# The second MLP product of five chunks: seven products instead of eight for the latents' two token tiles

## The chip, the cores and the metric

The kernel runs on one core of a Trainium2 chip. The metric is the device time of one execution in microseconds (us). Each time before is one of three runs; the profile is of one further execution of the same program.

## What is computed

The reference is one step of a flow-matching backbone: a token-mixing layer (an mLSTM and a pooling mixer), then an MLP. There are 128 prompt tokens and 256 latent tokens, D = 2048, and the MLP has 8192 hidden units. The change lies in the MLP:

```python
x = x + gate_a * _rmsnorm(mix, norm_w[1])
h = _rmsnorm(x, norm_w[2]) * (1 + scale_f) + shift_f
y = jnp.square(jax.nn.relu(h @ w1)) @ w2
x = x + gate_f * _rmsnorm(y, norm_w[3])
```

All of it is in fp32. The conditioning vectors (shift, scale, gate) are products of two vectors with a matrix of 2048 x 12288, one of which, gate_f, is worked out while the MLP runs.

## The kernel before

The 384 tokens are three token tiles of 128: tile 0 is the prompt, tiles 1 and 2 are the latents. TensorE multiplies in fp32r, a reduced format, so every operand is split into a high and a low part, hi and lo, and each product is three matmuls: high by high, high by low, low by high. For a weight tile this is `load_w`: a DMA brings 512 KB into a raw buffer (three of them), ScalarE copies it to hi (line 126), VectorE subtracts hi from raw to get lo (line 127); hi and lo have four buffers each.

The MLP runs in 8 chunks of 1024 hidden units (eight contraction tiles of w2). `gemm_T` on w1 makes a group of 256 hidden units, transposed: four loads, 24 matmuls of 384 columns for each (lines 135 to 137), and then for each of the two hidden tiles `evac_normed`: Relu on ScalarE (805), the square on VectorE (806), and `split_T` into hid high and low (181 and 182). `mlp_out(ch)` is the second product of a chunk: four blocks n of 512 output columns, in each four loads of two contraction tiles by 512 columns, and for each load 2 x 3 x 3 matmuls of 512 columns (901 to 903) with the hidden tile as the stationary operand, into three PSUM banks, one for each token tile. After a block three VectorE additions bring the banks into y (925; copies in chunk 0, 923).

The order is: one w1 group of the next chunk, the second product of this chunk, three more w1 groups. TensorE, ScalarE and VectorE each take their instructions in the order in which the scheduler has put them, which follows the order of the program and readiness. Side work is fed in between the loads by `Feed`: with rate r it takes r steps after each load. `ff` brings gate_f, at rate 0.2, so that it is spread from chunk 0 to chunk 6 (line 268 does its VectorE steps of 512 columns, one for each of the weight rows that a DMA has brought); `fx` stores an intermediate for the residual in chunk 0 (876), and `fn` (`norm_h2`) works the shift into h in chunk 0 (795 to 800). The last chunk ends with `last_part`, in which the third token tile's last 512 columns go in two halves of 256.

## Time and profile before

| | us |
|---|---|
| median of three runs (lowest, highest) | 1732.19 (1730.23, 1733.49) |
| the profiled execution's own time | 1733.51 |
| its span | 1731.8 |
| TensorE busy | 1693.1 |
| VectorE busy | 1082.6 |
| ScalarE busy | 629.1 |

Read it by stage: TensorE's share is an average over the token mixing, where it waits now and then, and the MLP, of which a table by stretches tells more than the page. In the stretches each number with (x) behind it is busy time and instructions of an engine, in the order of the first line; then come the granted TensorE clock (1.00 is the full one) and the DMA's share. In a timeline a matmul's length includes time in which the next already runs, so its cost is read from start to start.

### The profile page before, as it was taken

The numbers are of one execution on the slowest core, as the hardware profiler recorded it, in microseconds if no ns is written. First come the engines' busy times: TensorE is split into PE (matmuls) and PEld (weight loads), VectorE is DVE, ScalarE is ACT, GpSimd is POOL, SyncE is SP. The second block draws the span as 40 slices with busy tenths as digits, with TensorE's granted clock in tenths as the row PEclk, the third lists the DMA queues.
The fourth block names the chain that finished last, engine by engine and source line by source line (L and its number), as shares of the span: only waits on it lengthen the run. The fifth ranks groups of instructions, "written<-read, shape, count | busy, mean of one in ns | idle before, by whom it ended". The sixth has DMA issues, their size and how long they took to land.

```text
span 1731.8 us, 24241 instructions
## 1 busy us (share of the span) xinstructions
PE 1693.1 (98%) x9461; PEld 1527.8 (88%) x9461; DVE 1082.6 (63%) x1620; ACT 629.1 (36%) x1050; POOL 150.6 (9%) x186
## 2 busy tenths in 40 slices
PE   6999999999999999999999999999999999999997
PEld 3777899989999989989988988988988988998986
DVE  3676749898989959997347443466434344443446
ACT  4332345545433335553322332332332332332332
POOL 0000001221001224530000000000000000000100
PEclk9999999999999999999999999999999999999999
DMA  9978858777778894755446444454444445434543
GB/s 303 308 254 290 281 155 257 234 236 241 221 234 266 261 309 125 210 164 173 131 123 193 151 131 122 126 156 144 122 128 128 122 122 180 124 122 143 175 133 109
DMA packets 235266, 320.71 MB, mean 185 GB/s; under 512 B 14368, under 2 KB 177808, under 8 KB 234768
## 3 DMA queue, kind: packets, MB, share of 16 engines
q1 hardware_dynamic: 227760, 303.61, 56.1%
q0 software_dynamic: 5728, 13.69, 2.8%
...
q8 instruction: 74, 1.21, 0.3%
...
## 4 chain that ended last, share of the span: by engine, by line
PE 76%; DVE 9%; DMA 8%; issue 4%; ACT 1%; POOL 1%; SPq 0%; DVEq 0%; ACTq 0%; POOLq 0%
PE y L901 10%; PE y L903 10%; PE y L902 10%; PE acc_w L135 9%; PE acc_w L136 9%; PE acc_w L137 9%; DVE ada_acc L268 4%; DMA raw_u<-in_w_in_dram 3%; PE acc_o L135 1%; PE acc_o L137 1%; PE acc_o L136 1%; PE acc_q L135 1%; PE acc_q L137 1%; DMA raw_v<-in_w_in_dram 1%; PE acc_q L136 1%
## 5 line engine op out<-in xcount | busy, mean ns | idle before, releaser
L127 DVE TENSOR_TENSOR lo_w<-raw_w,hi_w 128x1024 fp32r<-128x1024 f32 x256 | 313.2, 1224 | 402.5 <-ACT hi_w L126 402.1
L126 ACT ACTIVATE hi_w<-raw_w 128x1024 fp32r<-128x1024 f32 x256 | 271.3, 1060 | 560.9 <-PE y L903 277.6
L136 PE MATMUL acc_w<-h2l,hi_w 128*128 128x384 f32 (+1 forms) x1024 | 345.8, 338 | 0.5 <-DVE h2l L857 0.5
L135 PE MATMUL acc_w<-h2h,hi_w 128*128 128x384 f32 (+1 forms) x1024 | 344.6, 338 | 1.6 <-ACT h2h L853 1.2
L137 PE MATMUL acc_w<-h2h,lo_w 128*128 128x384 f32 (+1 forms) x1024 | 345.4, 337 | 0.0
L268 DVE SCALAR_TENSOR_TENSOR ada_acc<-ada_raw,sg,ada_acc 128x1024 f32<-128x1024 f32 (+1 forms) x240 | 258.2, 1111 | 0.8 <-DMA ada_raw<-in_ada_w_dram 0.7
L135 PEld LDWEIGHTS acc_w<-h2h,hi_w 128*128 128x128 f32 x1024 | 192.2, 188 | 3.5 <-ACT h2h L853 2.0
L136 PEld LDWEIGHTS acc_w<-h2l,hi_w 128*128 128x128 f32 x1024 | 192.8, 188 | 1.8 <-DVE h2l L857 0.8
L137 PEld LDWEIGHTS acc_w<-h2h,lo_w 128*128 128x128 f32 x1024 | 192.5, 188 | 0.1
L806 DVE TENSOR_TENSOR z<-z 128x384 f32<-128x384 f32 x54 | 30.0, 555 | 53.4 <-ACT z L805 53.2
L126 ACT ACTIVATE hi_wo<-raw_wo 128x1024 fp32r<-128x1024 f32 x32 | 34.0, 1062 | 80.4 <-DMA raw_wo<-in_w_out_dram 57.6
L925 DVE TENSOR_TENSOR y<-y,y 128x512 f32<-128x512 f32 x81 | 55.5, 691 | 11.1 <-PE y L903 10.8
...
L805 ACT ACTIVATE z<-acc_w 128x384 f32<-128x384 f32 x54 | 26.3, 488 | 75.5 <-PE acc_w L137 75.5
L394 PE MATMUL v<-hi_v,hh 128*128 128x384 f32 (+1 forms) x144 | 49.0, 341 | 0.0
L395 PE MATMUL v<-lo_v,hh 128*128 128x384 f32 (+1 forms) x144 | 47.9, 332 | 0.0
L396 PE MATMUL v<-hi_v,hl 128*128 128x384 f32 (+1 forms) x144 | 47.8, 332 | 0.0
L221 PE MATMUL ada<-ada_raw,cT 128*32 128x256 f32 x672 | 45.7, 392 | 1.6 <-DMA ada_raw<-in_ada_w_dram 1.5
L127 DVE TENSOR_TENSOR lo_wo<-raw_wo,hi_wo 128x1024 fp32r<-128x1024 f32 x32 | 40.2, 1265 | 9.8 <-ACT hi_wo L126 9.7
L135 PE MATMUL acc_k<-hh,hi_k 128*128 128x384 f32 x128 | 44.4, 347 | 0.8 <-ACT C L603 0.8
L135 PE MATMUL acc_o<-hh,hi_o 128*128 128x384 f32 x128 | 44.1, 345 | 0.0
L135 PE MATMUL acc_q<-hh,hi_q 128*128 128x384 f32 x128 | 44.0, 343 | 0.0
...
## 6 DMA issues: line engine op xcount, KB each, us to landing
raw_w<-in_w_dram SPq DMA_DIRECT2D x256, 512.0 KB, 3.7
ada_raw<-in_ada_w_dram SPq DMA_DIRECT2D x188, 512.0 KB, 4.8
raw_wo<-in_w_out_dram SPq DMA_DIRECT2D x32, 512.0 KB, 5.1
raw_u<-in_w_in_dram SPq DMA_DIRECT2D x16, 512.0 KB, 8.8
raw_q<-in_w_in_dram SPq DMA_DIRECT2D x16, 512.0 KB, 5.1
raw_k<-in_w_in_dram SPq DMA_DIRECT2D x16, 512.0 KB, 5.0
raw_o<-in_w_in_dram SPq DMA_DIRECT2D x16, 512.0 KB, 4.9
...
```

The lines of the kernel that those rows point to most:

```text
L126: nc.scalar.activation(hi[:, 0:n], raw[:, 0:n], AF.Copy)
L127: low = lambda: nc.vector.tensor_tensor(lo[:, 0:n], raw[:, 0:n], hi[:, 0:n].bitcast(F32), op=ALU.subtract)
L135: nc.tensor.matmul(ps, lh, rh, start=start, stop=False)
L136: nc.tensor.matmul(ps, lh, rl, start=False, stop=False)
L137: mm3.ins = nc.tensor.matmul(ps, ll, rh, start=False, stop=stop).ins
L268: nc.vector.scalar_tensor_tensor(acc[:, g, :], raw[:, a, :], cj, acc[:, g, :], op0=ALU.mult, op1=ALU.add)
L394: nc.tensor.matmul(acc[i][:, 0:n], xh[:, sl], hi[:, k, :], start=k == 0, stop=False)
L395: nc.tensor.matmul(acc[i][:, 0:n], xh[:, sl], lo[:, k, :], start=False, stop=False)
L901: nc.tensor.matmul(acc, xh[:, s], hi, start=k == 8 * ch, stop=False)
L902: nc.tensor.matmul(acc, xh[:, s], lo, start=False, stop=False)
L903: nc.tensor.matmul(acc, xl[:, s], hi, start=False, stop=k == 8 * ch + 7)
L925: nc.vector.tensor_tensor(dst, acc[i], dst, op=ALU.add)
```

## The change

In chunks 2 to 6 the second product is no longer `mlp_out` but `mlp_seven`. For each pair of contraction tiles (an even and an odd one) and each pair of column halves (256 each) the latents' two token tiles form a 2 x 2 product of 2 x 2 blocks. Strassen's scheme (in Winograd's form) needs seven block products for it where the plain way needs eight; the prompt's tile stays plain and shares weight sums with them. So the loads become four tiles of 4 x 256 columns (b11, b21, b22, b12), three of seven weight operands are the raw tiles b11, b21, b22, and four are differences: t1 = b12 - b11, t3 = b22 - b12, t2 = b22 - t1, t4 = b21 - t2, worked out in place on VectorE. All seven are split into hi and lo. The hidden side's sums are made in `evac_pair`, with a third split (`hs`) for each pair of hidden tiles. A block has 132 matmuls of 256 columns instead of 72 of 512, five PSUM banks, and six additions into y and into two running sums r16 and r7, which `seven_done` folds into y after chunk 6.

To make room, gate_f is finished before chunk 2: its rate goes from 0.2 to 0.65, with buffers in a pool of its own that is closed there. The tail's buffers open in chunk 7, `z` has five buffers for two, and the masks and a few tiles move to other pools. Within a chunk from 2 on the order is: blocks 0 and 1, one w1 group, blocks 2 and 3, three w1 groups.

```diff
-N_X = 2
+N_X = 4
+RATE_GF = 0.65
+S_FIRST, S_LAST = 2, 6
...
+    def evac_pair(t, ps):
+
+        z = mlp.tile([P, NTOK], F32, tag="z", name=f"z{t}", bufs=5)
+        nc.scalar.activation(z, ps[:, 0:NTOK], AF.Relu)
+        nc.scalar.activation(z, z, AF.Square)
+        if t % 2 == 0:
+            z_even.append(z)
+            return
+        z0, s = z_even.pop(), mlp.tile([P, NTOK], F32, tag="z", name=f"s{t}", bufs=5)
+        a11, a21, a12, a22 = z0[:, P:2 * P], z0[:, 2 * P:], z[:, P:2 * P], z[:, 2 * P:]
+        s1, s2, s4 = (s[:, i * P:(i + 1) * P] for i in range(3))
+        tt = nc.vector.tensor_tensor
+        tt(s1, a21, a22, op=ALU.add)
+        tt(a21, a11, a21, op=ALU.subtract)
+        hid[t - 1], hid[t] = split_T(z0, f"hid{t - 1}"), split_T(z, f"hid{t}")
+        tt(s2, s1, a11, op=ALU.subtract)
+        tt(s4, a12, s2, op=ALU.subtract)
+        hid["s", t] = split_T(s, f"hs{t}")
...
-    fx, ff, fn = Feed(first_side(), 1.0), Feed(gate_late(), 0.2), Feed(norm_h2(), 1.0)
+    fx, ff, fn = Feed(first_side(), 1.0), Feed(gate_late(), RATE_GF), Feed(norm_h2(), 1.0)
...
+    def mlp_seven(ch, n, strp, r16, r7):
...
+        for m, (r, c) in enumerate(((0, 0), (1, 0), (1, 1), (0, 1))):
+            pool, tag = ((wp, "raw"), (strp, "raw2"))[m % 2]
+            raws[r, c] = pool.tile([P, 1024], F32, tag=tag, name=f"w2_{ch}_{n}_{r}{c}", bufs=3)
+            nc.sync.dma_start(raws[r, c].rearrange("p (j q) -> p j q", q=256),
+                              w2v[:, k0 + r:k0 + 8:2, c0 + 256 * c:c0 + 256 * c + 256])
...
+        def product(m, half, row, tok, w, start=True, stop=True, js=range(4)):
...
+                nc.tensor.matmul(acc, xh, wh, start=start and j == 0, stop=False)
+                nc.tensor.matmul(acc, xh, wl, start=False, stop=False)
+                nc.tensor.matmul(acc, xl, wh, start=False, stop=stop and j == 3)
...
+        wa, wb = split(b11, "b11"), split(b21, "b21")
+        for js in ((range(3), range(3, 4)) if n == 0 else (range(4),)):
+            product("x7", 0, 0, 0, wa, js=js)
+            product("16", 0, 0, 1, wa, js=js)
+            product("yz", 0, 1, 0, wb, js=js)
+            product("23", 0, 1, 1, wb, js=js)
+        tt(b11, b12, b11, op=ALU.subtract)
+        yx = ys[0].rearrange("p (a q) -> p a q", a=2)
+        tt(yx, banks["x7"][:, 0:256].unsqueeze(1).to_broadcast([P, 2, 256]), yx, op=ALU.add)
+        w = split(b22, "b22")
+        product("yz", 1, 1, 0, w, stop=False)
+        product("23", 1, 2, 2, w)
+        tt(b12, b22, b12, op=ALU.subtract)
+        w = split(b11, "t1")
+        product("yz", 1, 0, 0, w, start=False)
+        product("45", 1, 2, 0, w)
+        tt(b22, b22, b11, op=ALU.subtract)
+        w = split(b12, "t3")
+        product("x7", 1, 0, 2, w)
+        add(ys[1], "23")
+        tt(b21, b21, b22, op=ALU.subtract)
+        w = split(b22, "t2")
+        product("16", 1, 2, 1, w)
+        add(ys[0], "yz")
+        w = split(b21, "t4")
+        product("45", 0, 1, 2, w)
...
+            add(r7[:, n], "x7", 1)
+            add(r16[:, n], "16")
+        add(ys[2], "45")
...
+            if ch == S_FIRST:
+                ff.finish()
+                gate_scope.close()
...
+            for n in range(4):
+                mlp_seven(ch, n, strp, r16, r7)
+                if n == 1:
+                    w1_group(4 * ch + 4)
+            if ch == S_LAST:
+                for n in range(4):
+                    seven_done(n, r16, r7)
+                str_scope.close()
+            for g in range(1, 4):
+                w1_group(4 * ch + 4 + g)
```

How it moves instructions is seen at three places. On TensorE, the second product of a middle chunk before, where the second block begins (y_1_0 is the PSUM bank of token tile 0, hi_w_24 and lo_w_24 the split weights, hid24h and hid24l the hidden tile's parts):

```order
L901 MATMUL y_0_2_10557<-hi_w_30_0_10632,hid31h 128x512
L902 MATMUL y_0_2_10557<-lo_w_30_0_10633,hid31h 128x512
L903 MATMUL y_0_2_10557<-hi_w_30_0_10632,hid31l 128x512
L901 MATMUL y_1_0_10657<-hi_w_24_1_10662,hid24h 128x512
L902 MATMUL y_1_0_10657<-lo_w_24_1_10663,hid24h 128x512
L903 MATMUL y_1_0_10657<-hi_w_24_1_10662,hid24l 128x512
L901 MATMUL y_1_1_10658<-hi_w_24_1_10662,hid24h 128x512
L902 MATMUL y_1_1_10658<-lo_w_24_1_10663,hid24h 128x512
L903 MATMUL y_1_1_10658<-hi_w_24_1_10662,hid24l 128x512
```

The same engine after, at the end of the second block of chunk 4, where the products with t2 (bank 16) give way to those with t4 (bank 45):

```order
L1088 MATMUL y_1_16_12420<-hi_1_t_12557,hs37h 128x256
L1089 MATMUL y_1_16_12420<-lo_1_t_12558,hs37h 128x256
L1090 MATMUL y_1_16_12420<-hi_1_t_12557,hs37l 128x256
L1088 MATMUL y_1_16_12420<-hi_1_t_12557,hs39h 128x256
L1089 MATMUL y_1_16_12420<-lo_1_t_12558,hs39h 128x256
L1090 MATMUL y_1_16_12420<-hi_1_t_12557,hs39l 128x256
L1088 MATMUL y_1_45_12422<-hi_1_t_12574,hid33h 128x256
L1089 MATMUL y_1_45_12422<-lo_1_t_12575,hid33h 128x256
L1090 MATMUL y_1_45_12422<-hi_1_t_12574,hid33l 128x256
L1088 MATMUL y_1_45_12422<-hi_1_t_12574,hid35h 128x256
L1089 MATMUL y_1_45_12422<-lo_1_t_12575,hid35h 128x256
L1090 MATMUL y_1_45_12422<-hi_1_t_12574,hid35l 128x256
```

The matmuls are half as wide, and each group of three belongs to one of five banks.

On VectorE, a block before, around the additions of one block and the lo parts for the next:

```order
L925 TENSOR_TENSOR y_6313<-y_1_0_9671,y_6313 128x512
L925 TENSOR_TENSOR y_6314<-y_1_1_9672,y_6314 128x512
L925 TENSOR_TENSOR y_6315<-y_1_2_9673,y_6315 128x512
L127 TENSOR_TENSOR lo_w_22_2_9857<-raw_w_22_2_9854,hi_w_22_2_9856 128x1024
L127 TENSOR_TENSOR lo_w_16_3_9893<-raw_w_16_3_9890,hi_w_16_3_9892 128x1024
L127 TENSOR_TENSOR lo_w_18_3_9917<-raw_w_18_3_9914,hi_w_18_3_9916 128x1024
L127 TENSOR_TENSOR lo_w_20_3_9941<-raw_w_20_3_9938,hi_w_20_3_9940 128x1024
L925 TENSOR_TENSOR y_6313<-y_2_0_9779,y_6313 128x512
L925 TENSOR_TENSOR y_6314<-y_2_1_9780,y_6314 128x512
L925 TENSOR_TENSOR y_6315<-y_2_2_9781,y_6315 128x512
L127 TENSOR_TENSOR lo_w_22_3_9965<-raw_w_22_3_9962,hi_w_22_3_9964 128x1024
```

VectorE after, in the second block of chunk 4 (w_4_1_rc are raw tiles, in place of which the differences are written; lo_1_b and lo_1_t are lo parts of raw tiles and of differences):

```order
L1113 TENSOR_TENSOR w_4_1_01_12416<-w_4_1_11_12414,w_4_1_01_12416 128x1024
L1077 TENSOR_TENSOR lo_1_t_12511<-w_4_1_00_12410,hi_1_t_12510 128x1024
L1117 TENSOR_TENSOR w_4_1_11_12414<-w_4_1_11_12414,w_4_1_00_12410 128x1024
L1077 TENSOR_TENSOR lo_1_t_12540<-w_4_1_01_12416,hi_1_t_12539 128x1024
L1121 TENSOR_TENSOR w_4_1_10_12412<-w_4_1_10_12412,w_4_1_11_12414 128x1024
L1094 TENSOR_TENSOR y_6319<-y_1_23_12421,y_6319 128x512
L1077 TENSOR_TENSOR lo_1_t_12558<-w_4_1_11_12414,hi_1_t_12557 128x1024
L1094 TENSOR_TENSOR y_6318<-y_1_yz,y_6318 128x512
L1077 TENSOR_TENSOR lo_1_t_12575<-w_4_1_10_12412,hi_1_t_12574 128x1024
L132 TENSOR_TENSOR lo_w_5120_0_12598<-raw_w_5120_0_12595,hi_w_5120_0_12597 128x1024
L1094 TENSOR_TENSOR r_9598<-y_1_x_12418,r_9598 128x256
L1094 TENSOR_TENSOR r_9597<-y_1_16_12420,r_9597 128x512
```

Between two lo parts there stands now a difference or an addition from PSUM.

On VectorE in chunk 0's second product, before, around the lo part of the second load of block 2 (lo_w_2_2):

```order
L876 STREAM_TRANSPOSE x1b_7728<-mo_6305 128x384
L800 SCALAR_TENSOR_TENSOR h2l_6632<-h2n_7734,mod,h2h_6631 128x128
L800 SCALAR_TENSOR_TENSOR h2l_6632<-h2n_7734,mod,h2h_6631 128x256
L796 TENSOR_TENSOR h2n_7771<-h2n_7771,r2bc 128x384
L127 TENSOR_TENSOR lo_w_2_2_7781<-raw_w_2_2_7778,hi_w_2_2_7780 128x1024
L800 SCALAR_TENSOR_TENSOR h2l_6727<-h2n_7771,mod,h2h_6726 128x128
L795 TENSOR_TENSOR h2n_7802<-h2h_6743,h2l_6744 128x384
L800 SCALAR_TENSOR_TENSOR h2l_6727<-h2n_7771,mod,h2h_6726 128x256
L796 TENSOR_TENSOR h2n_7802<-h2n_7802,r2bc 128x384
L923 COPY y_6313<-y_1_0_7584 128x512
L923 COPY y_6314<-y_1_1_7585 128x512
L923 COPY y_6315<-y_1_2_7586 128x512
```

And after:

```order
L803 TENSOR_TENSOR h2n_7772<-h2n_7772,r2bc 128x384
L953 COPY y_6318<-y_1_0_7616 128x512
L953 COPY y_6319<-y_1_1_7617 128x512
L807 SCALAR_TENSOR_TENSOR h2l_6640<-h2n_7772,mod,h2h_6639 128x128
L807 SCALAR_TENSOR_TENSOR h2l_6640<-h2n_7772,mod,h2h_6639 128x256
L953 COPY y_6320<-y_1_2_7618 128x512
L273 SCALAR_TENSOR_TENSOR ada_acc_512_7335<-ada_raw_512_6_7723,sg,ada_acc_512_7335 128x512 x4
L802 TENSOR_TENSOR h2n_7815<-h2h_6734,h2l_6735 128x384
L132 TENSOR_TENSOR lo_w_2_2_7825<-raw_w_2_2_7822,hi_w_2_2_7824 128x1024
L803 TENSOR_TENSOR h2n_7815<-h2n_7815,r2bc 128x384
L273 SCALAR_TENSOR_TENSOR ada_acc_512_7335<-ada_raw_512_7_7809,sg,ada_acc_512_7335 128x512
L807 SCALAR_TENSOR_TENSOR h2l_6735<-h2n_7815,mod,h2h_6734 128x128
```

Here lo_w_2_2 has moved behind the copies of block 1 and behind four steps of the gate (ada_acc), and more of these steps follow it.

## Rows read from the trace of the kernel before

**Rows 1.** The page's header and its busy times by engine.

```profile
span 1731.8 us, 24241 instructions
PE 1693.1 (98%) x9461; PEld 1527.8 (88%) x9461; DVE 1082.6 (63%) x1620; ACT 629.1 (36%) x1050; POOL 150.6 (9%) x186
```

**Rows 2.** Table by stretches of the MLP, TensorE, VectorE and the rest.

```profile
core 0: us, PE busy (x) PEld busy (x) DVE busy (x) ACT busy (x) POOL busy (x), PEclk, DMA share, GB/s
729.40:796.30 66.90, 66.90 (x292) 54.49 (x291) 65.84 (x120) 31.39 (x54) 17.05 (x28) 1.00 0.62 178
796.30:864.66 68.36, 68.36 (x390) 68.12 (x389) 30.01 (x35) 22.35 (x29) 0.00 (x0) 1.00 0.47 140
864.66:931.30 66.64, 66.64 (x294) 53.49 (x294) 32.76 (x38) 18.67 (x21) 0.00 (x0) 1.00 0.44 133
931.30:998.00 66.70, 66.70 (x383) 66.52 (x382) 43.36 (x59) 22.10 (x28) 0.00 (x0) 1.00 0.58 182
...
1265.00:1332.00 67.00, 67.00 (x295) 54.90 (x294) 27.88 (x29) 18.60 (x21) 0.00 (x0) 1.00 0.42 126
```

**Rows 3.** Timeline of TensorE: start us, length us, instruction; starts of stages.

```profile
797.47 0.34 PE L135 MATMUL acc_w<-h2h,hi_w 128*128 128x384 f32 x1
...
864.66 0.39 PE L901 MATMUL y<-hi_w,hid8h 128*128 128x512 f32 x1
...
881.32 0.40 PE L901 MATMUL y<-hi_w,hid8h 128*128 128x512 f32 x1
```

**Rows 4.** Timeline at the kernel's end, 256-wide matmuls and their loads (PEld).

```profile
1716.53 0.28 PE L901 MATMUL y<-hi_w,hid56h 128*128 128x256 f32 x1
...
1716.65 0.19 PEld L903 LDWEIGHTS y<-hi_w,hid56l 128*128 128x128 f32 x1
...
1716.77 0.19 PEld L901 LDWEIGHTS y<-hi_w,hid57h 128*128 128x128 f32 x1
...
1722.11 0.28 PE L903 MATMUL y<-hi_w,hid63l 128*128 128x256 f32 x1
```

**Rows 5.** Instructions by line and shape, 864 to 1700 us: busy, mean ns.

```profile
L127 DVE TENSOR_TENSOR lo_w<-raw_w,hi_w 128x1024 fp32r<-128x1024 f32 x199 | 243.8, 1225 | 366.2 <-ACT hi_w L126 365.9
L126 ACT ACTIVATE hi_w<-raw_w 128x1024 fp32r<-128x1024 f32 x199 | 211.0, 1060 | 474.7 <-PE y L903 256.8 <-PE acc_w L136 170.7 <-DVE y L925 43.7
L925 DVE TENSOR_TENSOR y<-y,y 128x512 f32<-128x512 f32 x78 | 53.4, 691 | 10.6 <-PE y L903 10.4
```

**Rows 6.** Timeline of VectorE, dense place in chunk 1.

```profile
929.31 1.23 DVE L127 TENSOR_TENSOR lo_w<-raw_w,hi_w 128x1024 fp32r<-128x1024 f32 x1
930.45 0.75 DVE L268 SCALAR_TENSOR_TENSOR ada_acc<-ada_raw,sg,ada_acc 128x512 f32<-128x512 f32 x1
931.11 1.94 DVE L925 TENSOR_TENSOR y<-y,y 128x512 f32<-128x512 f32 x3
932.97 0.74 DVE L268 SCALAR_TENSOR_TENSOR ada_acc<-ada_raw,sg,ada_acc 128x512 f32<-128x512 f32 x1
```

**Rows 7.** Timeline of TensorE's start and VectorE, second product of chunk 0.

```profile
730.76 0.39 PE L901 MATMUL y<-hi_w,hid0h 128*128 128x512 f32 x1
...
759.88 1.21 DVE L127 TENSOR_TENSOR lo_w<-raw_w,hi_w 128x1024 fp32r<-128x1024 f32 x1
...
762.29 0.48 DVE L800 SCALAR_TENSOR_TENSOR h2l<-h2n,mod,h2h 128x256 fp32r<-128x256 f32 x1
762.68 0.55 DVE L796 TENSOR_TENSOR h2n<-h2n,r2bc 128x384 f32<-128x384 f32 x1
763.15 1.88 DVE L923 COPY y<-y 128x512 f32<-128x512 f32 x3
```

**Rows 8.** Timeline of ScalarE and VectorE at the seam into chunk 1.

```profile
866.14 0.48 ACT L805 ACTIVATE z<-acc_w 128x384 f32<-128x384 f32 x1
...
868.62 0.56 DVE L182 TENSOR_TENSOR hid17l<-z,hid17h 128x384 fp32r<-128x384 f32 x1 [0.59 <-ACT hid17h L181]
```

**Rows 9.** The page's DMA issues, w1 and w2, us to landing.

```profile
raw_w<-in_w_dram SPq DMA_DIRECT2D x256, 512.0 KB, 3.7
```

More of the change, by code (lines that the diff above doesn't have):

```diff
@@ L59, in bank @@
         return psum.tile([P, 512], F32, tag="ps", name=name)
-    cst = const.tile([P, N_CST, P], F32, name="cst")
+    cst = const.tile([P, 3, P], F32, name="cst")
     cs_src = consts.rearrange("p (n q) -> p n q", q=P)
@@ L70, in hymba_kernel @@
     prm = pre.tile([P, 2, P], F32, name="prm")
+    masks = vp.tile([P, N_CST - 3, P], F32, name="masks")
     nc.sync.dma_start(cc[:, 0, :], c_ctx.rearrange("(p j) -> p j", j=16))
@@ L224, in ada_mat @@
                     yield
-        sb = wp.tile([P, 512], F32, tag="adasb", name=f"ada_sb_{parts[0][0]}_{parts[0][1]}", bufs=1)
+        sb = adap[0].tile([P, 512], F32, tag="adasb", name=f"ada_sb_{parts[0][0]}_{parts[0][1]}", bufs=1)
         nc.scalar.activation(sb[:, 0:w], ps[:, 0:w], AF.Copy)
@@ L253, in load @@
         def load(t):
-            raw = wp.tile([P, nj, n], F32, tag="ada", name=f"ada_raw_{i}_{c}_{t}", bufs=N_ADA)
+            raw = adap[0].tile([P, nj, n], F32, tag="ada", name=f"ada_raw_{i}_{c}_{t}", bufs=N_ADA)
             nc.sync.dma_start(raw, aw[:, nj * t:nj * t + nj, c0:c0 + n])
@@ L313, in hymba_kernel @@
     xT = []
-    rbc = const.tile([P, NTOK], F32, name="rbc")
+    rbc = pre.tile([P, NTOK], F32, name="rbc")
     ss = const.tile([P, 3], F32, name="ss")
@@ L387, in hymba_kernel @@
                 with tc.issue_after(load_w.ins):
-                    nc.sync.dma_start(cst[:, 3:N_CST], cs_src[:, 3:N_CST])
+                    nc.sync.dma_start(masks, cs_src[:, 3:N_CST])
             acc = [bank(f"{kind}_{c0}_{s}_{i}") for i in range(3)]
@@ L424, in pooling @@
                     c0 = gi * 256 + ct * P
-                    nc.tensor.matmul(ps[:, i * P:(i + 1) * P], u_sb[i][:, c0:c0 + P], cst[:, (C_PC if i == 0 else C_PL) + gi, :], start=True, stop=True)
+                    nc.tensor.matmul(ps[:, i * P:(i + 1) * P], u_sb[i][:, c0:c0 + P], masks[:, (C_PC if i == 0 else C_PL) + gi - 3, :], start=True, stop=True)
                 ph.append(split_T(ps[:, 0:NTOK], f"p{gi}{ct}"))
@@ L479, in gates @@
                     elif part == 1:
-                        nc.tensor.matmul(ps_a[r, cols], lf[:, i, d, :], cst[:, tri[d][1], :], start=False, stop=True)
+                        nc.tensor.matmul(ps_a[r, cols], lf[:, i, d, :], masks[:, tri[d][1] - 3, :], start=False, stop=True)
                     else:
-                        nc.tensor.matmul(ps_b[r, cols], lf[:, i, d, :], cst[:, tri[d][0], :], start=True, stop=True)
+                        nc.tensor.matmul(ps_b[r, cols], lf[:, i, d, :], masks[:, tri[d][0] - 3, :], start=True, stop=True)
         for d in range(2):
@@ L768, in hymba_kernel @@
     vp_scope.close()
+    ada_scope.close()
     def token_rstd_rows(accs, name, between=None):
@@ L813, in gate_f @@
         for q in (1, 2, 3):
-            yield from ada_vec(5, 512 * q, 512, mlp)
+            yield from ada_vec(5, 512 * q, 512, adap[0])
         ps = bank("gfT")
-        t = mlp.tile([32, P], F32, name="gfT", bufs=1)
+        t = adap[0].tile([32, P], F32, name="gfT", bufs=1)
         nc.tensor.transpose(ps[0:32, 0:P], mod[:, 5].rearrange("p k g -> p (k g)"), ident)
@@ L874, in store_x1 @@
         for k in range(KT):
-            t = mlp.tile([P, NTOK], F32, tag="x1b", name=f"x1b{k}")
+            t = adap[0].tile([P, NTOK], F32, tag="x1b", name=f"x1b{k}", bufs=2)
             nc.vector.transpose(t, mo[k][:, 0:NTOK])
@@ L887, in evac_hid @@
     def evac_hid(t, ps):
-        z = mlp.tile([P, NTOK], F32, tag="z", name=f"z{t}")
+        z = mlp.tile([P, NTOK], F32, tag="z", name=f"z{t}", bufs=5)
         bz = mlp.tile([P, 2], F32, tag="bz", name=f"bz{t}")
@@ L965, in load_tail @@
     def load_tail():
+        tail = ctx.enter_context(tc.tile_pool(name="tail", bufs=1))
+        tails.append(tail)
         for g in range(2):
             for hf in range(2):
-                t = wp.tile([P, 1024], F32, tag="ada", name=f"gf{g}{hf}", bufs=N_ADA)
+                t = tail.tile([P, 1024], F32, name=f"gf{g}{hf}")
                 nc.gpsimd.dma_start(
@@ L981, in done @@
     def done(i, a, b, side=iter(())):
-        jk = mlp.tile([P, 512], F32, tag="jk", name=f"jky{i}_{a}", bufs=1)
+        jk = tails[0].tile([P, 512], F32, tag="jk", name=f"jky{i}_{a}", bufs=1)
         n = a // 512 + (a % 512 > 0)
@@ new lines, in seven_done @@
+    def seven_done(n, r16, r7):
+        tt = nc.vector.tensor_tensor
+        ys = [y[i][:, 512 * n:512 * n + 512] for i in range(3)]
+        r1, r6, v = r16[:, n, 0:256], r16[:, n, 256:], r7[:, n]
+        tt(ys[1][:, 0:256], ys[1][:, 0:256], r1, op=ALU.add)
+        tt(r6, r6, r1, op=ALU.add)
+        tt(v, v, r6, op=ALU.add)
+        tt(r6, r6, ys[2][:, 256:], op=ALU.add)
+        tt(ys[1][:, 256:], ys[1][:, 256:], r6, op=ALU.add)
+        y2 = ys[2].rearrange("p (a q) -> p a q", a=2)
+        tt(y2, y2, v.unsqueeze(1).to_broadcast([P, 2, 256]), op=ALU.add)
@@ new lines, in w1_group @@
+    def w1_group(g, feeds=(), n=NTOK):
+        ch = g // 4
+        evac = evac_hid if n == 386 else evac_pair if S_FIRST <= ch <= S_LAST else evac_normed
+        gemm_T(w1, [grp(g)], hx2, n, evac, feeds, name="w1")
+    for ch in range(8):
+        if ch < S_FIRST:
+            w1_group(4 * ch + 4, (ff, fx), 386 if ch == 0 else NTOK)
+            mlp_out(ch, (ff, fx, fn) if ch == 0 else (ff, fx))
+            if ch == 0:
+                fn.finish()
+            for g in range(1, 4):
+                w1_group(4 * ch + 4 + g, (ff,))
+        elif ch <= S_LAST:
+            if ch == S_FIRST:
+                ff.finish()
+                gate_scope.close()
+                str_scope = ExitStack()
+                strp = str_scope.enter_context(tc.tile_pool(name="strp", bufs=1))
+                r16, r7 = strp.tile([P, 4, 512], F32, name="r16"), strp.tile([P, 4, 256], F32, name="r7")
+            for n in range(4):
[6 more added lines that the diff above has]
+                str_scope.close()
+            for g in range(1, 4):
+                w1_group(4 * ch + 4 + g)
+        else:
+            load_tail()
+            ws = mlp_out(ch, (), done)
```

54 lines of the change are left out of this document (37 added, 17 removed).

## The prediction

> **What bounds the kernel now.** I read first the page's header and busy times: TensorE is busy 1693.1 of 1731.8 us, 98% [rows 1], so a change pays where it takes columns away from TensorE, and costs where it makes TensorE wait. The second view is the table by stretches, cut at the seams of the MLP: in the second product of chunk 0 (729.40 to 796.30), in the w1 groups after it, in the second product of chunk 1 and in the w1 groups after that, TensorE is busy for the whole length of the stretch, at a granted clock of 1.00 [rows 2]. There is no wait to remove there; the time of a stretch is its number of matmuls times their spacing. The same rows show who could become late: VectorE is busy 65.84 of 66.90 us in chunk 0, but only 32.76 of 66.64 in chunk 1, and 27.88 of 67.00 in chunk 4 [rows 2], whose seams the change rewrites.
>
> **The TensorE term (part one of the change).** Before, a block of w2 is 72 matmuls of 512 columns. The timeline gives the start of the first matmul of a block, 864.66, and of the first of the next, 881.32: 16.66 us for 72, 0.2314 us each [rows 3]. After, a block is 132 matmuls of 256 columns: 48 for the prompt (two contraction tiles x two column halves x four pairs x three) and 84 for the latents' seven products (7 x 4 x 3), where there were 96. In columns that is 33,792 for 36,864, 8.3% less. What a 256-wide matmul of the same three-product form takes is shown by the kernel's own end, where 48 run in a row: first start 1716.53, last start 1722.11, so 5.58 us / 47 = 0.1187 us [rows 4]. It is not quite half of 0.2314 (0.1157): a narrower matmul pays 3 ns more. A new block is 132 x 0.1187 = 15.67 us, 0.99 us less; there are five chunks of four blocks, so **-19.8 us**. If 256-wide matmuls kept the columns' price (0.1157) it would be 20 x (16.66 - 15.27) = -27.8; that is the far end on the good side, which the row denies.
>
> [...]
>
> **The VectorE term (part two).** A block before costs VectorE four subtractions of 1024 (lo parts) and three additions of 512 from PSUM. After it is eleven operations of 1024 (seven lo parts and four in-place differences of weights), five additions of 512 and one of 256. The trace holds two prices. The mean durations are 1225 and 691 ns [rows 5]: 11 x 1.225 + 5 x 0.691 + 0.48 (a 256-wide one [rows 7]) = 17.4 us. But where VectorE works without a gap, an operation starts before the end of the one ahead: 1.14 us from start to start after a 1024-wide one (929.31 to 930.45), and 1.86 for three PSUM additions (931.11 to 932.97), 0.62 each [rows 6], and 0.39 after a 256-wide one (762.29 to 762.68 [rows 7]): 11 x 1.14 + 5 x 0.62 + 0.39 = 16.0 us. TensorE's new block is 15.67. So the stage stands on a knife's edge: by the dense price VectorE loses 0.3 us a block, by the mean price 1.7. I take the dense price, since a busy VectorE is just the case of [rows 6].
>
> What absorbs the 0.3 is the order: two blocks, then a w1 group, two blocks, then three w1 groups. Four w1 groups of 96 matmuls each last from 797.47 to 864.66 [rows 3], 16.8 us a group and 0.175 us a matmul, and in each VectorE has four lo parts (4.6 us) and a pair of evacuations (about 2.7). So ahead of each pair of blocks VectorE can be early by as much as the four hi/lo buffers hold, about a load or two, 2 to 4 us. Stepping one pair through by hand with these prices I find the tightest place at the last product of the second block (t4, fourth in a chain of in-place differences), some 1.1 us early. No stall follows.
>
> The other new place is the seam into a chunk, where the last pair of hidden tiles has just been computed. Before, Relu of its last tile starts at 866.14, and its lo part starts at 868.62 and ends at 869.18, 4.5 us after the block's start at 864.66 [rows 3, 8]; now ScalarE does Relu and square, VectorE four sums of 128 columns, and a third split follows. The new first block works on three of its four pairs first, 36 matmuls, 4.3 us, before it reads that pair. By my steps the tiles are ready 3.5 to 5.05 us after the seam, needed at 4.3 and 5.0: 0 to 0.8 us lost, five times. The weights' landing, 3.7 us [rows 9], is covered by 4 us or more of earlier issue, but the second tile of the next block has only 2 us to spare. For this whole part I take **+1.0 us** (five seams at 0.2); its bounds are 0 and, if every second block of a pair ran at the mean price, 10 x (17.4 - 15.67) = +17.3, which is the first rival.
>
> **The chunk 0 term (part three).** The gate's steps were spread at rate 0.2 over chunks 0 to 6 and must now end before chunk 2, at 0.65. So 12 to 16 further steps of 0.66 us (930.45 to 931.11 [rows 6]), 8 to 10.6 us, fall into chunk 0's second product, where VectorE has 66.90 - 65.84 = 1.06 us free [rows 2]. They stand in VectorE's queue between the copies of block 1 and the lo parts of block 2. Before, the lo part of the second load of block 2 starts at 759.88; TensorE needs it at 730.76 + 9 x 4.17 = 768.3 [rows 7]. In the new order it stands behind the three copies, which begin at 763.15 [rows 7] since they wait for block 1, then four gate steps (2.6), a sum (0.5) and the subtraction itself (1.2). With the backlog of 5 to 9 us from the steps further up I get 770.5, a stall of 2.0; the next load's loses 1.2 more. What waits there is TensorE, and nothing makes that up: **+3.2 us**, bounds 0 (the backlog eaten by the 8 us of lead) and 7 (10.6 us less the smallest lead that I found). Chunk 1 takes steps too, but VectorE is busy for half of it only [rows 2].
>
> **Edits at nothing.** The final folding of the two extra sums (twenty additions of 256, four of 512, about 10 us) runs under three w1 groups of 16.8 each after chunk 6; if that cover were gone it would be up to 10 us at once. The DMA bytes stay as they are, with DMA busy at 0.42 to 0.62 [rows 2]. Pools that move (masks, gate tiles, tail tiles) move no instruction before the MLP that I could find.
>
> **Sum**: -19.8 + 1.0 + 3.2 = -15.6. The profiled execution's own span of 1731.8 becomes 1716.2; its time, 1733.51, lies 1.3 above the median of the three runs, 1732.19, so I set the change against the median: 1732.19 - 15.6 = **1716.6 us**.
>
> **The rivals.** *VectorE sets the pace of the second block of each pair*, at its mean price, without any lead: 10 x (17.4 - 15.67) = +17.3 in place of +1.0, and the time is 1732.19 - 19.8 + 17.3 + 3.2 = 1732.9, no change. For it speaks that the lead is only four buffers; against it, [rows 6]. [...]
>
> *VectorE sets the pace of every block*, the slower side: the chain of differences and lo parts is serial (a difference waits for the lo part that still reads its tile, the lo part for ScalarE's copy of 1.06 us [rows 5], that copy for the difference). If such waits put the block at 17.4 us throughout, with no help from the w1 groups, 20 x (17.4 - 16.66) = +14.8, +3.2 for chunk 0, and the time is 1750.2. It decides from a VectorE block of 16.66 us on, only 0.7 above my dense sum. Against it: VectorE has twice the needed time in each w1 group.
>
> *The weight loads set the pace.* A load lasts 0.19 us [rows 4], longer than the 0.1187 between two 256-wide matmuls. If loads ran one after another, 132 x 0.19 = 25.1 us a block, 20 x (25.1 - 16.66) = +169, 1904 us. The rows speak against it: loads start at 1716.65 and 1716.77, each 0.19 long, so two are under way at once over 48 matmuls [rows 4], and the w1 matmuls run at 0.175, under a load's length too. [...]
>
> **How the numbers follow.** My forecast, with both small terms between their bounds: 0.79, giving 1711 (all of the small terms at nothing give 1712.4) to 1727 (three times the seam term and 7 us in chunk 0 give 1722.4, and some 4 us for a VectorE that falls behind in part of the pairs). First rival 0.08, second 0.07, third 0.01; 0.05 for a mixture that ends between 1727 and 1733. A measurement of this kernel can tell 0.2%, 3.5 us, from no change: faster means below 1728.7, slower above 1735.7. The range that holds 8 in 10 is 1711 to 1728. Faster 0.84 (the forecast and most of the mixture), same 0.08, slower 0.08.
>
> **What would show it.** In the trace after: a block of chunks 2 to 6 of 15.67 us with starts 0.119 apart; VectorE busy nearly throughout in the pairs, at 1.14 from start to start; waits of TensorE for lo parts of 2 to 4 us at about 768 to 774, in chunk 0, and under 1 us at the five seams. I am wrong if the last difference's split (t4) is waited for in each second block, if the 256-wide matmuls in w2 are spaced wider than at the kernel's end, or if chunk 0 shows no wait at all.

## The result and the profile after

The changed kernel takes 1718.68 us (median of four runs, 1715.41 to 1720.39) against 1732.84 for the kernel before on the same chip. The ratio is 0.9914, 95% interval 0.9888 to 0.9939: 14.2 us less, where 15.6 were forecast. Two later measurements gave 0.9903 (0.9886 to 0.9921) and 0.9904 (0.9887 to 0.9921) for the same kernel, about 17 us. One execution of this kernel (2340 us) and one of a kernel further down (6546 us) ran in a far slower state; all medians and ratios here are of the fast runs. The profiled execution after is the fastest of the first four runs (1715.41), and the one of before is a little above its median, so the two spans lie further apart than the medians: 1731.8 - 1713.4 = 18.4 us. The account below is of these 18.4.

The page's header and busy times after, to be read against [rows 1]:

```profile
span 1713.4 us, 27071 instructions
PE 1673.3 (98%) x10661; PEld 1567.0 (91%) x10661; DVE 1284.6 (75%) x1900; ACT 721.9 (42%) x1178; POOL 150.3 (9%) x186
```

TensorE issues 1200 matmuls more and is busy for 20 us less. VectorE takes 202 us more work.

The table by stretches, cut at the same seams as [rows 2]: the second product of chunk 0, the w1 groups after it, the second product of chunk 1, then, in chunk 3, the first and the second block of a pair, and last the whole of chunks 2 to 6.

```profile
core 0: us, PE busy (x) PEld busy (x) DVE busy (x) ACT busy (x) POOL busy (x), PEclk, DMA share, GB/s
730.66:803.59 72.93, 69.88 (x301) 55.69 (x301) 68.36 (x129) 31.86 (x55) 17.09 (x28) 0.98 0.58 170
803.59:871.82 68.23, 68.23 (x398) 67.56 (x396) 55.31 (x78) 22.76 (x30) 0.00 (x0) 1.00 0.64 205
871.82:939.85 68.03, 68.03 (x301) 54.63 (x301) 42.38 (x60) 20.02 (x24) 0.00 (x0) 1.00 0.44 140
...
1119.54:1135.18 15.64, 15.64 (x133) 15.64 (x133) 12.92 (x19) 10.05 (x14) 0.00 (x0) 1.00 0.45 135
1135.18:1150.77 15.59, 15.59 (x134) 15.59 (x133) 15.59 (x18) 6.57 (x7) 0.00 (x0) 1.00 0.38 112
...
990.22:1636.91 646.69, 646.69 (x4562) 646.69 (x4561) 473.35 (x564) 291.87 (x360) 13.24 (x22) 1.00 0.45 138
```

Chunks 2 to 6 take 646.69 us, in which TensorE does not wait once. The same five chunks before, in one stretch of its table:

```profile
983.03:1655.33 672.30, 672.30 (x3386) 607.51 (x3386) 299.47 (x341) 204.34 (x243) 13.68 (x23) 1.00 0.45 137
```

So the account is: chunks 2 to 6, 672.30 to 646.69, **-25.6**; the second product of chunk 0, which was 66.72 (730.76 to 797.47 [rows 3, 7]), **+6.2**; from there to the start of chunk 2, 185.56 (797.47 to 983.03) to 186.63 (803.59 to 990.22), **+1.1**. What lies ahead of chunk 0's second product comes out even, 730.76 to 730.66, but only as the sum of two differences: from the end of the token mixing (the matmuls on `sqa`) it is 97.00 us before and 100.47 after, **+3.5**, while the mixing itself ended 3.6 us earlier in the profile after, 630.19 for 633.76. The sum is -18.4.

The 3.6 are no part of what the change does, as far as can be seen: in the twelve profiles of kernels that have the gate's new pool the mixing ends between 630.2 and 639.7, and 633.76 lies among them. Without them the change is worth 14.8 us by the profiles, and this agrees with the medians, 14.2 to 17.

The +3.5 is a wait at the seam into the MLP that all twelve have. TensorE, before and then after:

```profile
633.76 0.72 PE L776 MATMUL tr_r<-cst,sqa 128*128 128x1 f32 x6
...
641.15 0.97 PE L135 MATMUL acc_w<-h2h,hi_w 128*128 128x386 f32 x4 [0.53 <-ACT h2h L853]
```

```profile
630.19 0.72 PE L782 MATMUL tr_r<-cst,sqa 128*128 128x1 f32 x6
...
640.86 0.64 PE L226 MATMUL ada<-y,cT 128*32 128x256 f32 x8 [0.40 <-DMA y<-in_ada_w_dram]
641.43 0.98 PE L140 MATMUL acc_w<-h2h,hi_w 128*128 128x386 f32 x4
```

From the first of these matmuls to the first w1 matmul it is 7.4 us before, 11.2 after, and 11.0 to 12.8 in the twelve. Between them stand gate_f's first 64 matmuls, and their loads come later now. SyncE's issue of the first of them, before and then after:

```profile
601.44 0.38 SPq L217 DMA_DIRECT2D ada_raw<-in_ada_w_dram  x1
```

```profile
616.75 3.95 SPq L222 DMA_DIRECT2D ada_raw<-in_ada_w_dram  x4
```

And a row of the list of what SyncE's queue waited for, 596 to 645 us, after (sum, times, longest):

```profile
SPq L222 <- PE adav L284: 1.1, 1, 1.1
```

Before, these loads go into a pool that is open throughout, and the first is issued at 601.44. After, they go into the gate's own pool, which the program opens where an earlier one is closed; the first waits for TensorE's `adav`, a step of the vector worked out before the gate (done at 616.64), and is issued at 616.75. That the pool is the reason is read from the program and these rows; no run moves the gate back alone.

Start of the first and end of the last matmul of a pair of blocks (chunk 2), by the timeline of TensorE:

```profile
990.22 0.28 PE L1088 MATMUL y_x<-hi_b,hid16h 128*128 128x256 f32 x1
...
1021.37 0.33 PE L140 MATMUL acc_w<-h2h,hi_w 128*128 128x384 f32 x1
```

31.15 us for 264 matmuls is 0.1180 each, 15.57 a block. The ten pairs lie between 31.11 and 31.23.

VectorE in the second block of a pair (timeline of chunk 3): the operations stand close, and the price from start to start is 1.13 to 1.14 us after one of 1024 and 0.60 after an addition of 512.

```profile
1142.30 1.22 DVE L1077 TENSOR_TENSOR lo_t<-w,hi_t 128x1024 fp32r<-128x1024 f32 x1
1143.43 1.22 DVE L1121 TENSOR_TENSOR w<-w,w 128x1024 f32<-128x1024 f32 x1
1144.57 0.68 DVE L1094 TENSOR_TENSOR y<-y,y 128x512 f32<-128x512 f32 x1
1145.17 1.21 DVE L1077 TENSOR_TENSOR lo_t<-w,hi_t 128x1024 fp32r<-128x1024 f32 x1
```

In that block VectorE is busy for 15.59 of 15.59 us, and TensorE still runs through: the lo part of the last product (t4) is ready 1.3 to 1.4 us before the matmul that reads it first, in chunks 3 to 6.

The only wait of TensorE in the MLP's second products is in chunk 0. TensorE's timeline there (in brackets the idle time ahead and what ended it):

```profile
768.25 0.86 PE L931 MATMUL y<-hi_w,hid2h 128*128 128x512 f32 x3
772.17 0.50 PE L932 MATMUL y<-lo_w,hid2h 128*128 128x512 f32 x1 [3.05 <-DVE lo_w L132]
...
773.70 0.63 PE L931 MATMUL y<-hi_w,hid3h 128*128 128x512 f32 x1
774.12 0.63 PE L932 MATMUL y<-lo_w,hid3h 128*128 128x512 f32 x1
```

And VectorE's queue ahead of that lo part: the last copy of block 1, four steps of the gate, a sum, the subtraction.

```profile
767.17 0.68 DVE L953 COPY y<-y 128x512 f32<-128x512 f32 x1
767.78 2.73 DVE L273 SCALAR_TENSOR_TENSOR ada_acc<-ada_raw,sg,ada_acc 128x512 f32<-128x512 f32 x4
770.42 0.56 DVE L802 TENSOR_TENSOR h2n<-h2h,h2l 128x384 f32<-128x384 f32 x1
770.89 1.22 DVE L132 TENSOR_TENSOR lo_w<-raw_w,hi_w 128x1024 fp32r<-128x1024 f32 x1
```

The part is ready at 772.1. Behind the wait the matmuls start 0.42 us apart (773.70 to 774.12) instead of 0.23: the granted clock, 0.98 over the whole stretch, is 0.50 from 773.70 to 776.90. Of the 6.2 us, 3.05 are the wait and 0.9 the gate's own 12 matmuls, which stood in a later stage before; eight or nine matmuls at half the clock, 0.19 us longer each, are an estimated 1.6.

### The profile page after: what moved, and what is told of

Read it like the earlier page. It is cut to its first block, busy times and chain, and to the rows that moved or that the text cites. A ratio compares the mean times of both kernels' runs of the same rounds, so it can differ in the third digit from the quotient of the medians.

```text
span 1713.4 us, 27071 instructions
## 1 busy us (share of the span) xinstructions
PE 1673.3 (98%) x10661; PEld 1567.0 (91%) x10661; DVE 1284.6 (75%) x1900; ACT 721.9 (42%) x1178; POOL 150.3 (9%) x186
## 4 chain that ended last, share of the span: by engine, by line
PE 85%; DVE 6%; DMA 5%; issue 2%; ACT 1%; SPq 1%; POOL 0%; DVEq 0%; ACTq 0%; POOLq 0%
PE acc_w L140 10%; PE acc_w L141 10%; PE acc_w L142 10%; PE y L932 4%; PE y L931 3%; PE y L933 3%; PE y L1089 3%; PE y L1090 3%; PE y L1088 3%; DVE ada_acc L273 2%; DMA raw_u<-in_w_in_dram 2%; PE acc_wo L140 2%; PE acc_wo L142 2%; PE acc_wo L141 2%; PE y_yz L1089 2%
## 5 line engine op out<-in xcount | busy, mean ns | idle before, releaser
L132 DVE TENSOR_TENSOR lo_w<-raw_w,hi_w 128x1024 fp32r<-128x1024 f32 x176 | 215.2, 1224 | 192.9 <-ACT hi_w L131 191.0
L131 ACT ACTIVATE hi_w<-raw_w 128x1024 fp32r<-128x1024 f32 x176 | 186.5, 1060 | 304.3 <-PE acc_w L141 97.2
L1076 ACT ACTIVATE hi_t<-w 128x1024 fp32r<-128x1024 f32 x80 | 84.4, 1061 | 87.2 <-PE y L1090 23.5
L1077 DVE TENSOR_TENSOR lo_t<-w,hi_t 128x1024 fp32r<-128x1024 f32 x80 | 97.4, 1223 | 11.7 <-ACT hi_t L1076 11.3
L1077 DVE TENSOR_TENSOR lo_b<-w,hi_b 128x1024 fp32r<-128x1024 f32 x60 | 73.3, 1222 | 35.3 <-ACT hi_b L1076 35.3
L1076 ACT ACTIVATE hi_b<-w 128x1024 fp32r<-128x1024 f32 x60 | 63.7, 1061 | 77.1 <-PE acc_w L141 51.3
L1002 POOL DMA_DIRECT2D gf<-gf_dram x4 | 3.6, 898 | 649.8 <-DVE y L1146 649.8
```

The source lines that it names most:

```text
L131: nc.scalar.activation(hi[:, 0:n], raw[:, 0:n], AF.Copy)
L132: low = lambda: nc.vector.tensor_tensor(lo[:, 0:n], raw[:, 0:n], hi[:, 0:n].bitcast(F32), op=ALU.subtract)
L1076: nc.scalar.activation(hi, raw, AF.Copy)
L1077: nc.vector.tensor_tensor(lo, raw, hi.bitcast(F32), op=ALU.subtract)
```

## The experiments

The theory: in chunks 2 to 6 TensorE alone sets the time, so the saving is matmuls taken away times 0.118 us, less the dearer halves; VectorE is near its limit but covered; and the gate's earlier steps cost a few us in chunk 0. The rivals: VectorE or the loads set a part of the pace, or the loss in chunk 0 is chance.

**The changed kernel again** (no edit).

> The changed kernel once more, unaltered, to see which parts of its profile come back. Theory: the wait of TensorE for the second load of block 2 in chunk 0 (3.0 us) is there again, since the order of the instructions makes it, and with it a stretch of a few us at half the clock right behind; the ten pairs of blocks take 31.1 to 31.2 us each. Span 1713 to 1718. Rival: the wait or the half clock was chance; then chunk 0's second product is 67 to 70 us instead of 72.9.

Measured: 1717.71 us (five runs), ratio 0.9903. The wait is 2.4 us, at the same load; chunk 0's second product takes 72.1; the half clock is there again; the ten pairs are the same to 0.02 us. The pattern comes back, so chance is out as an explanation.

**The gate's half of the change alone.** Chunks 2 to 6 take the plain second product.

```diff
-        evac = evac_hid if n == 386 else evac_pair if S_FIRST <= ch <= S_LAST else evac_normed
+        evac = evac_hid if n == 386 else evac_normed
...
-            for n in range(4):
-                mlp_seven(ch, n, strp, r16, r7)
-                if n == 1:
-                    w1_group(4 * ch + 4)
...
+            w1_group(4 * ch + 4)
+            mlp_out(ch)
             for g in range(1, 4):
                 w1_group(4 * ch + 4 + g)
```

> Only the other half of the change: the gate at rate 0.65 and finished before chunk 2, the new pools, but in chunks 2 to 6 the plain second product with 72 matmuls of 512 columns a block, and the old order of the w1 groups. Theory: chunks 0 and 1 are 6 to 7 us longer than before, as in the changed kernel, and chunks 2 to 6 are shorter by the 1 to 2 us that the gate's own matmuls took there; 4 to 6 us slower than before, 1737 to 1739. The seven products then carry about -24. Rival: the gate costs nothing by itself and the wait in chunk 0 is due to other moves; then it is within 1 us of before.

Measured: 1740.21 us, ratio 1.0036 (1.0022 to 1.005), some 6 us slower than before. Its table: chunk 0's second product, one plain second product, the four w1 groups behind it, and chunks 2 to 6.

```profile
733.33:805.10 71.77, 68.39 (x301) 54.55 (x301) 68.87 (x130) 31.68 (x55) 17.04 (x28) 1.00 0.60 174
1008.49:1075.32 66.83, 66.83 (x289) 54.08 (x289) 29.07 (x31) 18.36 (x20) 0.00 (x0) 1.00 0.42 126
1075.32:1142.34 67.02, 67.02 (x386) 67.02 (x385) 26.66 (x30) 22.46 (x29) 0.00 (x0) 1.00 0.43 126
...
991.73:1660.97 669.24, 669.24 (x3362) 605.51 (x3361) 278.62 (x300) 204.09 (x241) 9.62 (x18) 1.00 0.43 131
```

This splits the -25.6: without the gate the five chunks take 669.24, 3.1 less than before (24 matmuls fewer, which with the gaps around them take 1.9 us in the timeline before; the other 1.2 is not traced); the seven products take them from 669.24 to 646.69, **-22.6**, or 1.13 us a block: 66.83 / 4 = 16.71 against 15.57. The medians say the same, 1740.21 - 1717.71 = 22.5. Moving the gate is a loss of its own: +6.1 in chunks 0 and 1 and +3.8 at the seam into the MLP (11.2 us for 7.4) against -3.1 later, 6.8 us by the trace and 5.7 by the medians.

**Eight products.** One of the seven is worked out twice.

```diff
-        product("45", 1, 2, 0, w)
+        for _ in range(2):
+            product("45", 1, 2, 0, w)
```

> In each of the twenty new blocks one of the seven products (the one with t1 for the bank 45) is worked out twice, so TensorE does eight products, 144 matmuls of 256 columns, while VectorE and ScalarE do what they did. Theory (TensorE alone sets the time of these blocks): 20 x 12 x 0.118 = +28.3 us against the changed kernel, a pair of blocks 34.0 us; about 10 us slower than before. Rival (VectorE or the loads set a part of the pace): less than +25.

Measured: 1747.33 us, ratio 1.0083 (1.0058 to 1.0108), 29.6 over the changed kernel beside it. A pair in its table:

```profile
991.18:1025.13 33.95, 33.95 (x290) 33.95 (x289) 27.46 (x32) 18.62 (x25) 0.00 (x0) 1.00 0.43 128
```

2.80 us more for 24 matmuls, 0.117 each: in these blocks TensorE pays for each added matmul in full (0.118 apart in the changed kernel), and nothing else has a share. A block of 144 narrow matmuls is 33.95 / 2 = 16.98 us, 0.27 more than 72 wide ones (16.71): over twenty blocks the narrow form alone loses 5.4 us, and leaving out the eighth product wins 28.

**No gate steps fed between the loads of chunk 0's second product.**

```diff
-RATE_GF = 0.65
+RATE_GF = 0.8
...
-            mlp_out(ch, (ff, fx, fn) if ch == 0 else (ff, fx))
+            mlp_out(ch, (fx, fn) if ch == 0 else (ff, fx))
```

> The gate's steps are no longer fed between the loads of chunk 0's second product; elsewhere their rate goes from 0.65 to 0.8, so that they still end before chunk 2. Theory (steps of the gate in front of the lo part make TensorE wait, and the wait brings the half clock): both go, chunk 0's second product falls from 72.9 to about 67 us, the kernel by 4.5 to 6 us against the changed kernel of the same call. Rival (the wait comes from elsewhere, such as the copies of block 1 or a late landing): it stays, within 1 us. A second rival: the w1 groups of chunk 0, in which VectorE gets more steps, become late instead, and the gain is under 2 us.

Measured: 1714.99 us beside 1717.71, ratio 0.9888 (0.9867 to 0.9909). Gate steps that were fed earlier or later still run in the stage, 14 of them (15 before, 21 in the changed kernel), but none from 735 to 787 us, where the lo part in question stands. The wait is gone, and the stage is back at its length before (66.72):

```profile
734.77:801.58 66.81, 66.81 (x289) 54.08 (x289) 65.79 (x120) 31.32 (x54) 17.04 (x28) 1.00 0.60 177
```

The steps in front of the lo part made the wait. The gain by the median is 2.7, less than the 5.3 of the stage: the gate's last quarter now falls into chunk 1's w1 groups (51.62 for 50.38), and the stages ahead of the MLP differ by several us between runs. So it was taken once more, beside the changed kernel on one chip.

> The kernel without gate steps in chunk 0's second product once more, beside the changed kernel on the same chip. Theory: 4 us faster than the changed kernel by the stages up to chunk 2 (344.4 us from the first w1 group for 348.5), 2 to 4.5 by the median. Rival: the stages from run to run differ as much, and the medians are within 1 us.

> The changed kernel, unaltered, on the same chip, 1716 to 1719 us. The wait in chunk 0 is 2 to 3 us again; whether the half clock follows it is open, since three of the earlier profiles with such a wait show none.

Measured: 1717.01 and 1717.98, ratios 0.9881 (0.986 to 0.9901) and 0.9904 (0.9887 to 0.9921). From the first w1 group to chunk 2 it is 344.1 us (648.06 to 992.17) against 349.1 (643.70 to 992.80), but the mixing ended 5.2 us later in this profile than in that of the changed kernel. Both times this kernel is ahead of the changed kernel, by 2.7 and 1.0 us, and of the kernel before by 19 and 18; its interval overlaps that of the changed kernel, so that the gain over the latter is clear in the stage only.

**More work for VectorE.** One, two or four of a block's lo parts are made twice, here one:

```diff
-            nc.vector.tensor_tensor(lo, raw, hi.bitcast(F32), op=ALU.subtract)
+            for _ in range(2 if name in ("b22",) else 1):
+                nc.vector.tensor_tensor(lo, raw, hi.bitcast(F32), op=ALU.subtract)
```

> In each new block VectorE makes one lo part (of b22) twice: one more operation of 1024 a block, 1.14 us. Theory A (the w1 groups and the buffers give slack): in the changed kernel VectorE has 2.7 us without work in a pair of blocks (28.5 busy of 31.2) and the last lo part (t4 of the second block) is ready 1.3 us ahead; together 4.0 us, and 2.3 us a pair are added, so nothing is lost: 0 to +3 us against the changed kernel, pairs stay at 31.2. Rival B (the idle time lies where the buffers are full and cannot be used; only the 1.3 us count): 2.3 - 1.3 = 1.0 us a pair, +10 us, pairs of 32.2 us. Rival C (VectorE at its mean duration of 1.22 us, 17.4 a block, is the bound already): +23 us.

> Two lo parts twice in each block (b21 and b22), 4.6 us more VectorE work in a pair. A: 4.6 - 4.0 = 0.6 us a pair, +6 us. B: 4.6 - 1.3 = 3.3 us a pair, +33 us. C: +46 us.

> Four lo parts twice in each block (b11, b21, b22, t1), 9.1 us more VectorE work in a pair. A: 9.1 - 4.0 = 5.1 us a pair, +51 us. B: 9.1 - 1.3 = 7.8 us a pair, +78 us. C: +91 us. In all three TensorE now waits for lo parts in each pair, and the slope from two to four is 4.5 us a pair, VectorE's start-to-start price.

Measured: 1729.53 us (ratio 0.9973, 0.9956 to 0.999), 1741.15 (1.0036, 1.0019 to 1.0053) and 1772.52 (one run). The ten pairs are longer by 4.8, 15 and 40 us in all, so 0.5, 1.5 and 4.0 a pair, where A had 0, 0.6 and 5.1, B 1.0, 3.3 and 7.8, and C 2.3, 4.6 and 9.1. A is nearest and C is out, but none of the three is right in its numbers, and the slope from two to four is 2.5 a pair, not 4.5. So VectorE's slack is not one fixed reserve; where the rest of it is found, these runs do not show. Where TensorE waits is seen with two extra operations. The list of TensorE's waits from 990 us on has two rows (sum, times, longest):

```profile
PE y_x L1089 <- ACT hi_t L1076: 10.5, 10, 1.5
PE acc_w L142 <- DVE lo_w L132: 3.8, 1, 3.8
```

The first is once in each pair; the second comes up again below. The timelines of VectorE, ScalarE and TensorE in such a second block:

```profile
1145.03 1.22 DVE L1114 TENSOR_TENSOR w<-w,w 128x1024 f32<-128x1024 f32 x1
...
1146.42 1.06 ACT L1076 ACTIVATE hi_t<-w 128x1024 fp32r<-128x1024 f32 x1 [1.86 <-DVE w L1114]
...
1147.53 0.39 PE L1089 MATMUL y_x<-hi_t,hid24h 128*128 128x256 f32 x1 [1.16 <-ACT hi_t L1076]
```

The difference t3 waits its turn on VectorE, ScalarE copies it, and TensorE, at its end, starts 0.05 us after the copy. The late thing is the chain from a difference through the hi copy, not the lo part.

The rest of the loss with one extra operation (11.8 us over the changed kernel's 1717.7, of which 4.8 in the pairs) is one event, at the end of chunk 6. TensorE's only wait from 990 us on:

```profile
PE acc_w L142 <- DVE lo_w L132: 4.0, 1, 4.0
```

And the table's row for the three w1 groups there, 50.26 us in the changed kernel:

```profile
1595.49:1652.44 56.95, 52.93 (x290) 52.61 (x289) 26.67 (x35) 17.28 (x22) 13.20 (x22) 0.94 0.70 224
```

A wait of 4.0 us and a granted clock of 0.94. In VectorE's timeline there ten additions of the final folding stand ahead of the lo part, which starts at 1599.10. The next runs show in another kernel what these do.

**Four blocks in a row.** The w1 group is moved from between the pairs to behind them.

```diff
             for n in range(4):
                 mlp_seven(ch, n, strp, r16, r7)
-                if n == 1:
-                    w1_group(4 * ch + 4)
...
-            for g in range(1, 4):
+            for g in range(4):
                 w1_group(4 * ch + 4 + g)
```

> In chunks 2 to 6 the four blocks stand in a row, and the w1 group that stood between the pairs follows them. Theory: VectorE needs 16.0 us a block at its start-to-start prices against TensorE's 15.6, so the lead of the last lo part falls by about 0.4 a block after the second: 1.3, 0.9, 0.5 us; no wait, four blocks in 62.3 us, within 2 us of the changed kernel. Rival (only the w1 group between the pairs keeps VectorE up): the third and fourth block wait 0.5 us or more each, +5 us or more over the five chunks.

Measured: 1729.14 us, ratio 0.9975 (0.9956 to 0.9994), 11 over the changed kernel's 1717.7. The blocks did as the theory said: four in a row take 62.3 us, and in chunk 3 t4's lead is 3.3, 1.4, 1.1 and 0.9 us. The loss is again at the end of chunk 6. The table's rows for that chunk's blocks and for the four groups behind them:

```profile
1511.37:1573.70 62.33, 62.33 (x530) 62.33 (x529) 59.43 (x71) 31.23 (x35) 0.00 (x0) 1.00 0.35 111
1573.70:1650.19 76.49, 68.58 (x387) 68.26 (x385) 37.85 (x54) 23.33 (x30) 13.24 (x22) 0.96 0.63 195
```

The list of TensorE's waits from 990 us on:

```profile
PE acc_w L142 <- DVE lo_w L132: 7.9, 1, 7.9
```

And VectorE's timeline there, the first row of the folding, the last ahead of the lo part that TensorE lacks, and that lo part:

```profile
1571.83 0.42 DVE L1140 TENSOR_TENSOR y<-y,r 128x256 f32<-128x256 f32 x1
...
1580.86 0.42 DVE L1142 TENSOR_TENSOR r<-r,r 128x256 f32<-128x256 f32 x1
1581.19 1.22 DVE L132 TENSOR_TENSOR lo_w<-raw_w,hi_w 128x1024 fp32r<-128x1024 f32 x1
```

From 1571.83 on VectorE folds the running sums; 21 of the 24 additions stand ahead of the first group's lo part in its queue. In the changed kernel the lo parts of the group stand between them: the first starts at 1584.98, and the folding ends at 1594.7.

**The same with the folding spread**, one block of it behind each of the four groups. Against the run before:

```diff
-                for n in range(4):
-                    seven_done(n, r16, r7)
...
             for g in range(4):
                 w1_group(4 * ch + 4 + g)
+                if ch == S_LAST:
+                    seven_done(g, r16, r7)
```

> Four blocks in a row as in the run before, but the folding of the two running sums after chunk 6 is written one block behind each of the four w1 groups, no longer all of it ahead of them. Theory (the 7.9 us wait of that run and the half clock behind it came from the folding in front of the first group's lo parts, nothing from the missing w1 group): the four groups after chunk 6 fall from 76.5 to about 67 us, and the kernel comes to the changed kernel's time, within 2 us. Rival: VectorE is behind by more than the folding, a wait of 3 us or more stays at the same place.

Measured: 1717.83 us, ratio 0.9898 (0.9883 to 0.9913), the changed kernel's time. The four groups:

```profile
1569.63:1636.64 67.01, 67.01 (x386) 67.01 (x385) 37.57 (x55) 23.47 (x30) 13.20 (x22) 1.00 0.71 222
```

76.49 became 67.01, with the same VectorE work in the stretch. So the folding's place made all of that loss, and the w1 group between the pairs is worth nothing measurable.

## Why the prediction was right, and where its terms were off

The forecast, 1716.6, lies 2.1 below the measured median, and the range holds the median. The main term and its mechanism are right; that the total is so close is partly luck, as the end of this section shows. Step by step:

**The bound.** That TensorE's matmuls are the time of chunks 2 to 6 is shown: TensorE has no idle time there in either kernel (busy 672.30 of 672.30 us before, 646.69 of 646.69 after), and an eighth product costs its full price (0.117 us a matmul).

**The TensorE term**, forecast -19.8, is -22.6. The step that was mis-sized is the two spacings: 0.1187 was read from the 48 matmuls at the kernel's end, and 264 in a row take 0.1180; 0.2314 was read from one block, and 66.83 / 288 is 0.2320. Both errors go the same way, 0.14 us a block together.

**The VectorE term**, forecast +1.0, is nothing. The price was right: 1.13 to 1.14 from start to start, and the second block's VectorE is busy for its whole length. The tightest place, t4 of the second block, was forecast 1.1 us early and is 1.3. The seams cost nothing either: in chunk 3 the last pair's lo parts begin at 1123.24 and 1123.71 in VectorE's timeline, and the first matmuls that read them start at 1124.06 and 1124.78.

```profile
1123.24 0.56 DVE L187 TENSOR_TENSOR hid30l<-z,hid30h 128x384 fp32r<-128x384 f32 x1
1123.71 0.55 DVE L187 TENSOR_TENSOR hid31l<-z,hid31h 128x384 fp32r<-128x384 f32 x1
...
1124.06 0.28 PE L1090 MATMUL y_x<-hi_b,hid30l 128*128 128x256 f32 x1
...
1124.78 0.28 PE L1090 MATMUL y_yz<-hi_b,hid31l 128*128 128x256 f32 x1
```

They end 4.3 and 4.7 us after the seam at 1119.54, inside the forecast 3.5 to 5.05, and 0.3 and 0.5 ahead of need. What was wrong is the reason given for the cover: the w1 group between the pairs isn't needed, as four blocks in a row show.

**The chunk 0 term**, forecast +3.2, is +6.2 in this profile, 4.5 to 6.2 over the ten profiles of kernels that have the gate steps there. The wait came at the load that was named, 2.1 to 3.0 us long, ready at 772.1 where 770.5 was forecast; the second wait of 1.2 for a lo part did not come. Two things were missing: the half clock behind the wait (granted 0.50 for 3.2 us), and the gate's own matmuls, which came into chunks 0 and 1 and left chunks 2 to 6 (-3.1 there, not in my sum). And the count was off: 12 to 16 further gate steps were put into that stage, but there are 21 for 15, while most went on into the w1 groups behind it, where VectorE's busy time rose from 30.01 [rows 2] to 55.31 us. Six further steps were enough, since four of them stand in the queue just ahead of the lo part.

**Edits at nothing.** The folding did cost nothing, with its price in reserve named ("up to 10 us at once"): where other work displaced it, it took 9.5 (76.49 - 67.01). My cover was the length of three w1 groups; the cover that counts is the order in VectorE's queue. The pools that move were the wrong entry here: they "move no instruction before the MLP that I could find", but gate_f's first loads are issued 15 us later (616.75 for 601.44), and TensorE comes to the first w1 matmul 3.6 to 5.4 us later after the mixing than in the profile before. It is the largest term that the sum left out.

**The rivals.** VectorE at its mean duration is out: 17.4 us a block would be 34.8 a pair, and a pair takes 31.2. The weight loads are out too: they are 0.19 us long and TensorE goes at 0.118, with loads under way during all of the 646.69 us. That VectorE sets the pace of every block needed 0.7 us more in a block by my bound; one operation more (1.14) made the pairs 0.5 us longer, two (2.3) 1.5. The whole change turns into a loss between one and two further operations a block.

The errors fell on both sides. In this profile they are -2.8 for the spacings and -1.0 for VectorE, -2.0 between chunk 0's second product and the end of chunk 6 for the gate's matmuls and what is not traced (+1.1 and -3.1), against +3.0 in chunk 0 and +3.5 ahead of it: together 0.7. By the medians the saving is 1.4 below the forecast in the first measurement and 1.2 and 1.7 above it in the later two. Misses of 1 to 3.5 us each cancelled, and that is luck.
